# Residues of the weights on VectorE instead of GpSimd while the scans run

## The chip, the cores and the metric

The kernel runs on one core of one Trainium2 chip. The metric is the device time of one execution in microseconds; three runs of the kernel before gave a median of 2983.45 us (2982.43 to 2989.89). Engines are named as in the profile: PE is TensorE's matmuls, PEld its weight loads, DVE is VectorE, ACT is ScalarE, POOL is GpSimd, SP is SyncE, which here only issues DMAs.

## The reference, cut to what matters

One layer of a bidirectional backbone is computed for 1024 latent tokens and 128 context tokens, all in float32, with D_MODEL = 1024:

```
h = rmsnorm(x) * (1 + sc1) + sh1
z = h @ w_in                                  # r, k, v, low-rank inputs, conv inputs, gates
o_a = rwkv_mixer(r, k, v, ...)                # 16 heads x 64, one scan forward, one backward
o_b = cb * seq_conv(cc * cx)                  # gated short convolution
merged = g_a * (o_a @ w_pa) + g_b * (o_b @ w_pb)
x = x + gt1 * (merged @ w_o)
h2 = rmsnorm(x) * (1 + sc2) + sh2
u = seq_conv(h2 @ w_up);  x = x + gt2 * ((silu(u_act) * u_lin) @ w_down)
```

The outputs are the normalised tokens and the final states of the context scans. The scan's step is s = s * w + (s a) b + v k, y = s r, for every head and direction.

## The kernel before, in words

All 1152 tokens are worked on together, in three column tiles of 384. Every large product is a "dense job": one tile of 128 output channels, weights of 8 x 128x128 in two halves of 128x512. TensorE multiplies operands of type `fp32r`, and the kernel keeps float32's precision by splitting each operand in a high part and a residue: `hi` is a copy of the weights to that format (ScalarE, `whi<-wraw`), `lo` is `wraw - hi` (`wlo<-wraw,whi`, the subject of this document), and a product is three matmuls, `hi*hi + hi*lo + lo*hi`. A half's way is: DMA from HBM to `wraw` (issued on GpSimd's queue, two buffers), `whi` on ScalarE, `wlo` (three buffers each), then matmuls. `split_w` records copy and residue, one half at the end of a job's first column tile and one within its last, for the job that comes next.

The jobs stand in one list. First come the products with w_in (`psd<-h` in the profile), 67 tiles and a product with the low-rank gate; then those with w_pb (`psd<-x`), for which the convolution branch is read back and split. A second list has w_pa (`psd<-x` too), after which come w_o (`psd<-mg`), w_up (`psd<-g`) and w_down (`psd<-a`).

Between the matmuls of the first list the scans are woven in. They are cut in 36 items (four pairs of head pairs, nine pieces of 128 tokens). An item's work is a set of streams: `prep` (decays and scaled keys: tiles `thw`, `ak`, `fa`, `bt`, `krk`), `prep2` (Gram matrices `gpb` and `gpk` on TensorE, masked by VectorE into `G`, `E` and `O`), `chain` (a triangular inverse: 31 steps of two VectorE operations, `Xt<-X,Dm` and `X<-X,Xt`, on blocks that a DMA brings as `Dm`), `merge` (`mps`, `RSt`), `scan` (matmuls `px` and `py`, state `Wt`) and `finish` (norm of the head's output, `fps`, `fb`, `fv`, `fg`, `y`). What these need and give goes through HBM by DMAs on SP's queue.

What sets the order is a planner in the program itself. `Clock` has a time `now`, which each matmul moves on by a cost, and one time for each of VectorE ("V"), ScalarE ("A") and GpSimd ("G"). Every recorded instruction adds its cost to its engine's time; a stream goes on when the clock has reached the end of its last piece, and `prep` and `finish` only if the backlog of VectorE and ScalarE is under 1500 or 1000 ns. So a cost that is charged to another engine moves what comes after it on all of them. A scheduler then keeps the order by priorities. The costs of the operation in question, from `tt`, and the place where the engine of the residue is chosen, from `split_w`, `split_eng` and `dense`:

```
s.use(eng, 127 + 1.05 * fsize(out) if eng == "V" else 204 + 2.3 * fsize(out))
...
self.tt(s, lo[:, :nk, :], raw[:, :nk, :], hi[:, :nk, :].bitcast(F32), ALU.subtract, eng=self.split_eng())
...
return self.split
...
self.split = self.split_next          # in dense(), after the first job's two halves
```

The first job's halves go to `split`, the others of that list to `split_next`. After the first list the program sets both to "V" (`K.split = K.split_next = "V"`).

Of the kernel before, what the change touches and what calls it, by code (L numbers as in the profile page):

```python
# [46 lines left out]
class Clock:  # L47


    def __init__(self):  # L50
        self.now = 0.0
        self.e = {"V": 0.0, "A": 0.0, "G": 0.0}
# [24 lines left out]
class Kern:  # L77
    def __init__(self, tc, ins, outs):
        self.tc, self.nc = tc, tc.nc
        self.ins, self.outs = ins, outs  # L80
        self.clk = Clock()
        self.streams = []
        self.events = set()
        self.split, self.split_next = "V", "G"


    def mm(self, out, lhsT, rhs, start, stop, cost):
# [1445 lines left out]
```

## Time and profile before

| | |
|---|---|
| median of three runs | 2983.45 us |
| profiled execution, its own time | 2987.0 us |
| its span in the profile | 2985.1 us |
| mean granted TensorE clock | 0.975 |
| busy: TensorE / weight loads | 2769.4 us (93%) / 2514.1 us (84%) |
| busy: VectorE, ScalarE, GpSimd | 2012.6 us (67%), 1267.4 us (42%), 494.4 us (17%) |
| residues of weights on VectorE / GpSimd | 186 / 148 |
| first and last residue on GpSimd | 13.6 us, 1906.0 us |
| last matmul with w_in | 1805.7 us |

Matmuls are pipelined and their ends are modelled, so a busy TensorE is not one at its peak. A row of groups shows the line, engine, operation, the tiles written and read, partitions x elements, the count, the busy time, the mean of one in ns, and the idle time of the engine ahead of it with what ended it. L110 is the helper `tt`, L105 `act`, L122 `stt`, L89 `mm`, L128 `dma`: most operations have a helper's line, so they are told apart by tiles. A wait is put down to what came last by the profile.

### The profile page before, as it was taken

To read this page: it belongs to the slowest core of one execution; us is meant where nothing else is said; L and a number is where in the kernel's file an instruction comes from. 1 tells how busy PE (TensorE), PEld (TensorE's weight loads), DVE (VectorE), ACT (ScalarE), POOL (GpSimd) and SP (SyncE) were. 2 spreads that over 40 slices of the span, in tenths; PEclk is the share of its full clock that TensorE was granted. 3 is DMA by queue.
4 is the path that set the end of the run, shared out by engine and by line. 5 is a ranking of instruction groups with operands and counts; after the bars stand their busy time and mean duration, and the time that the engine had idled before them with its cause. 6 is when DMAs were issued, how large, how long until landed. Compare 5 with 4: busy or idle time off the path is not lost. (4 is left out here: it accounts for less than half of the span.)

```text
span 2985.1 us, 63295 instructions
## 1 busy us (share of the span) xinstructions
PE 2769.4 (93%) x24762; PEld 2514.1 (84%) x24762; DVE 2012.6 (67%) x5039; ACT 1267.4 (42%) x2544; POOL 494.4 (17%) x678
## 2 busy tenths in 40 slices
PE   7896998999989999889999998999999999999997
PEld 3884887878778777777777788899999999999996
DVE  7457785687667689888887857955555454555556
ACT  4474645555454634334543454123443241424243
POOL 3211121121221111111111112200001101010101
PEclk9997999999999999999999999999999999999998
DMA  4577646466565645545554538843211111111112
GB/s 195 163 238 224 199 148 194 154 175 183 156 185 145 216 109 126 131 109 134 140 139 108 136 115 311 264 141 98 65 43 36 50 40 46 41 41 43 40 44 80
DMA packets 402641, 388.49 MB, mean 130 GB/s; under 512 B 189478, under 2 KB 354214, under 8 KB 402342
## 3 DMA queue, kind: packets, MB, share of 16 engines
q1 hardware_dynamic: 331174, 280.08, 31.1%
q0 software_dynamic: 32000, 99.65, 11.0%
q10 hardware_dynamic: 39168, 4.73, 1.1%
q8 instruction: 195, 3.19, 0.5%
q14 instruction: 104, 0.84, 0.1%
HBM read 268.17 MB, written 116.13 MB: 129 GB/s over the span
## 5 line engine op out<-in xcount | busy, mean ns | idle before, releaser
L89 PE MATMUL psd<-h,whi 128*128 128x384 f32 x3216 | 907.7, 353 | 17.2 <-ACT h L105 9.3
L89 PEld LDWEIGHTS psd<-h,whi 128*128 128x128 f32 x3216 | 591.8, 192 | 52.6 <-issue 12.6
L89 PE MATMUL psd<-h,wlo 128*128 128x384 f32 x1608 | 564.9, 351 | 1.3 <-POOL wlo L110 1.3
L89 PE MATMUL psd<-g,whi 128*128 128x384 f32 (+1 forms) x2112 | 543.2, 338 | 0.0
L105 ACT ACTIVATE whi<-wraw 128x512 fp32r<-128x512 f32 (+2 forms) x334 | 198.3, 594 | 494.3 <-PE psd L89 431.4
L89 PEld LDWEIGHTS psd<-g,whi 128*128 128x128 f32 x2112 | 383.5, 188 | 0.3
L110 POOL TENSOR_TENSOR wlo<-wraw,whi 128x512 fp32r<-128x512 f32 x148 | 199.7, 1350 | 1098.6 <-ACT whi L105 950.9
L89 PE MATMUL psd<-g,wlo 128*128 128x384 f32 (+1 forms) x1056 | 355.9, 337 | 0.0
L89 PEld LDWEIGHTS psd<-h,wlo 128*128 128x128 f32 x1608 | 309.0, 192 | 14.5 <-issue 5.3
L110 DVE TENSOR_TENSOR Xt<-X,Dm 128x60 f32<-128x60 f32 (+24 forms) x1116 | 258.8, 234 | 28.7 <-DMA Dm<-Dd 1.1
L110 DVE TENSOR_TENSOR X<-X,Xt 128x60 f32<-128x60 f32 (+24 forms) x1116 | 253.0, 229 | 27.4 <-DMA O<-fa 0.3
L89 PE MATMUL psd<-a,whi 128*128 128x384 f32 x864 | 218.9, 334 | 0.0
L89 PE MATMUL psd<-x,whi 128*128 128x384 f32 x768 | 200.2, 341 | 10.4 <-ACT x L105 6.7
L89 PEld LDWEIGHTS psd<-g,wlo 128*128 128x128 f32 x1056 | 199.3, 189 | 0.0
L110 DVE TENSOR_TENSOR wlo<-wraw,whi 128x512 fp32r<-128x512 f32 (+2 forms) x186 | 113.7, 611 | 110.6 <-ACT whi L105 110.6
L89 PEld LDWEIGHTS psd<-a,whi 128*128 128x128 f32 x864 | 156.0, 188 | 0.0
L110 DVE TENSOR_TENSOR fu<-psd,rs 128x384 f32<-128x384 f32 x132 | 73.4, 556 | 117.6 <-PE psd L89 105.1
L89 PEld LDWEIGHTS psd<-x,whi 128*128 128x128 f32 x768 | 140.9, 191 | 13.1 <-ACT x L105 7.0
L89 PE MATMUL psd<-a,wlo 128*128 128x384 f32 x432 | 144.0, 334 | 0.0
L122 DVE SCALAR_TENSOR_TENSOR x<-psd,mod,x 128x384 f32<-128x384 f32 (+3 forms) x160 | 79.1, 514 | 94.0 <-PE psd L89 93.9
L105 ACT ACTIVATE BK<-BK,PC 128x128 f32<-128x128 f32 x288 | 94.4, 391 | 108.1 <-PE gpk L89 86.2
L89 PE MATMUL psd<-x,wlo 128*128 128x384 f32 x384 | 130.4, 340 | 4.4 <-DVE wlo L110 4.4
(213 smaller groups left out, 5111.6 us busy)
## 6 DMA issues: line engine op xcount, KB each, us to landing
wraw<-in_w_in POOLq DMA_DIRECT2D x134, 256.0 KB, 3.5
wraw<-in_w_up POOLq DMA_DIRECT2D x88, 256.0 KB, 2.9
llo<-lo SPq DMA_DIRECT2D x98, 192.0 KB, 3.0
BK<-fb SPq DMA_DIRECT2D x36, 512.0 KB, 5.0
Dm<-Dd POOLq DMA_DIRECT2D x144, 128.0 KB, 3.6
wx<-in_wmb SPq DMA_DIRECT2D x32, 512.0 KB, 5.3
fa<-fa SPq DMA_DIRECT2D x40, 384.0 KB, 2.7
fb<-ak SPq DMA_DIRECT2D x40, 384.0 KB, 3.2
```

The lines of the kernel that those rows point to most:

```text
L89: return self.nc.tensor.matmul(out, lhsT=lhsT, rhs=rhs, start=start, stop=stop)
L105: self.nc.scalar.activation(out, in_, func, bias=bias, scale=scale)
L110: e.tensor_tensor(out, a, b, op)
L122: self.nc.vector.scalar_tensor_tensor(out, a, sc, b, op0, op1)
```

## The change

One value is changed: the engine of the residues after the first job of the first list.

```diff
@@ -81,7 +81,7 @@
         self.clk = Clock()
         self.streams = []
         self.events = set()
-        self.split, self.split_next = "V", "G"
+        self.split, self.split_next = "V", "V"
```

All 334 residues are VectorE's then. The planner charges each of the moved ones to VectorE's clock, with VectorE's cost, and so the order of all engines changes from early in the first list on. The number of instructions on the other engines stays, apart from how rows fall together.

On VectorE's queue, in the middle of the scans, the chain of the fifth item (tiles `X` and `Xt`; `cot` is the convolution branch). Before, and with the change:

```order
L110 TENSOR_TENSOR X<-X,Xt 128x28
L110 TENSOR_TENSOR Xt<-X,Dm 128x2x27
L110 TENSOR_TENSOR X<-X,Xt 128x2x27
L110 TENSOR_TENSOR Xt<-X,Dm 128x2x26
L110 TENSOR_TENSOR X<-X,Xt 128x2x26
L110 TENSOR_TENSOR Xt<-X,Dm 128x2x25
```

```order
L110 TENSOR_TENSOR X<-X,Xt 128x28
L110 TENSOR_TENSOR Xt<-X,Dm 128x2x27
L110 TENSOR_TENSOR X<-X,Xt 128x2x27
L110 TENSOR_TENSOR wlo<-wraw,whi 128x512
L110 TENSOR_TENSOR Xt<-X,Dm 128x2x26
L110 TENSOR_TENSOR X<-X,Xt 128x2x26
L110 TENSOR_TENSOR Xt<-X,Dm 128x2x25
```

A residue now stands between two steps of the chain, and what is behind it waits for its `whi`.

On VectorE's queue, at the end of the scans, where the work of `finish` for the last item meets the residues of the activations for w_pb and w_pa (tiles `x`; 17497 and 16655 are of the convolution branch for w_pb, 23256 to 23268 of the scans' output for w_pa) and the modulation's dot products (`wx`). Before, and with the change:

```order
L122 SCALAR_TENSOR_TENSOR fb<-fps,fb 128x128
L122 SCALAR_TENSOR_TENSOR y<-y,par,fb 128x128
L122 SCALAR_TENSOR_TENSOR y<-y,par,fv 128x128
L110 TENSOR_TENSOR fg<-y,fg 128x128
L396 SCALAR_TENSOR_TENSOR wx,mod<-wx 128x1024 x4
L110 TENSOR_TENSOR x_23256<-x_23256,x_23255 128x384 x3
L110 TENSOR_TENSOR x_23259<-x_23259,x_23258 128x384 x3
L110 TENSOR_TENSOR x_23262<-x_23262,x_23261 128x384 x3
L110 TENSOR_TENSOR x_23265<-x_23265,x_23264 128x384 x3
L110 TENSOR_TENSOR x_23268<-x_23268,x_23267 128x384 x3
L110 TENSOR_TENSOR x_17497<-x_17497,x_17496 128x384 x3
```

```order
L122 SCALAR_TENSOR_TENSOR fps<-fps,fb 128x128
L110 TENSOR_TENSOR wlo<-wraw,whi 128x512
L122 SCALAR_TENSOR_TENSOR fb<-fps,fb 128x128
L122 SCALAR_TENSOR_TENSOR y<-y,par,fb 128x128
L110 TENSOR_TENSOR wlo<-wraw,whi 128x512
L110 TENSOR_TENSOR x_16655<-x_16655,x_16654 128x384 x3
L122 SCALAR_TENSOR_TENSOR y<-y,par,fv 128x128
```

The scans end later against the dense jobs: `wx` and the w_pa residues no longer stand ahead of the w_pb residues, but two weight residues do. On TensorE's queue 121 matmuls with w_in stood behind the last matmul of `finish`, and 19 stand there now.

## The prediction

> **What bounds the kernel now.** I read the time by stretches first. The columns are busy time and count of TensorE (PE), its weight loads (PEld), VectorE (DVE), ScalarE (ACT) and GpSimd (POOL), then the granted clock:
>
> ```profile
> core 0: us, PE busy (x) PEld busy (x) DVE busy (x) ACT busy (x) POOL busy (x), PEclk, DMA share, GB/s
> 0.00:200.00 200.00, 165.72 (x712) 127.42 (x713) 120.06 (x194) 105.56 (x191) 56.72 (x66) 0.93 0.56 192
> 200.00:1000.00 800.00, 716.93 (x6716) 627.68 (x6714) 561.78 (x1453) 421.38 (x907) 154.70 (x188) 0.96 0.60 180
> 1000.00:1600.00 600.00, 544.94 (x8401) 454.08 (x8401) 508.01 (x1787) 244.00 (x573) 103.68 (x152) 0.98 0.51 133
> 1600.00:1910.00 310.00, 288.32 (x2960) 260.26 (x2961) 239.64 (x633) 123.46 (x245) 68.98 (x80) 0.97 0.61 190
> 1910.00:2985.00 1075.00, 1053.50 (x5980) 1044.64 (x5978) 583.12 (x977) 372.99 (x628) 110.35 (x192) 0.99 0.20 63
> ```
>
> TensorE is the bound everywhere. From 1910 us on nothing changes: its residues are VectorE's already, and it is 98% full. The change acts ahead of that. In 200 to 1910 us TensorE is idle for 83.1 + 55.1 + 21.7 = 159.9 us; a gain can come from there alone. VectorE is busy for 1309.4 of these 1710 us, idle for 401; it is fullest at 1000 to 1600 us, with 92 us idle in 600. Next, who waits for whom there (total, times, longest); the first rows of TensorE's, then VectorE's and GpSimd's last ones:
>
> ```profile
> PE gpk L89 <- DVE G L110: 16.5, 11, 4.1
> PE px L89 <- DVE Wt L1387: 14.8, 30, 2.3
> PE gpb L89 <- DMA BK<-fb: 14.3, 4, 7.8
> PE gpb L89 <- DMA E<-fa: 13.2, 11, 3.4
> PE lps L89 <- ACT ak L105: 6.8, 3, 3.6
> ...
> PE psd L89 <- POOL wlo L110: 1.3, 1, 1.3
> ...
> PE fps L89 <- DVE y L110: 0.3, 1, 0.3
> ```
>
> All of the view's rows for this stretch add up to 51.8 us for VectorE (20 rows, the first and the last of them above), 50.8 for ScalarE, 44.3 for DMAs, and 1.3 for a GpSimd residue. So the slow residues on GpSimd cost no wait worth naming: what the change can win is not there. It can only make VectorE earlier or later for TensorE.
>
> **The change, part by part.** *Added.* VectorE takes 148 subtractions of 128x512. What one costs there, and what it costs GpSimd, from the groups of the whole run; below them the same tile by stretch (TensorE's use, its loads, VectorE, GpSimd):
>
> ```profile
> L110 DVE TENSOR_TENSOR wlo<-wraw,whi 128x512 fp32r<-128x512 f32 x122 | 84.7, 694 | 80.3 <-ACT whi L105 80.3
> L110 POOL TENSOR_TENSOR wlo<-wraw,whi 128x512 fp32r<-128x512 f32 x148 | 199.7, 1350 | 1098.6 <-ACT whi L105 950.9 <-PE px L89 50.1 <-ACT BK L105 23.2
> 200.00:1000.00 800.00, 282.99 (x813) 155.85 (x812) 0.00 (x0) 91.83 (x68) 0.96 0.60 180
> 1000.00:1600.00 600.00, 147.87 (x411) 78.47 (x411) 0.00 (x0) 44.20 (x34) 0.98 0.51 133
> 1600.00:1910.00 310.00, 127.95 (x374) 70.95 (x374) 0.00 (x0) 43.28 (x31) 0.97 0.61 190
> ```
>
> 148 x 0.694 = 102.7 us more work on VectorE; 133 of the 148 lie in 200 to 1910 us.
>
> *Removed.* GpSimd's 199.7 us, and with them what they do to VectorE. One place in order of time (start, duration), GpSimd's row and then VectorE's:
>
> ```profile
> 702.78 1.29 POOL L110 TENSOR_TENSOR wlo<-wraw,whi 128x512 fp32r<-128x512 f32 x1
> 702.36 0.55 DVE L122 SCALAR_TENSOR_TENSOR kr<-ksq,kr 128x384 f32<-128x384 f32 x1
> 702.83 1.31 DVE L110 TENSOR_TENSOR Xt<-X,Dm 128x52 f32<-128x52 f32 x1
> 704.60 0.20 DVE L110 TENSOR_TENSOR X<-X,Xt 128x52 f32<-128x52 f32 x1
> ```
>
> The step Xt, which starts 0.05 us after the residue, takes 1.31 us and ends 0.07 us after it; its neighbour of the same size takes 0.20. Two operands in SBUF were held up until GpSimd was done. How much that is in all has bounds: nothing, and the 199.7 us for which GpSimd works on residues. Between them, the two operations of the chain (minimum, median and maximum, then the group's mean), and an operation of 128x1024 first beside GpSimd's residues (1830 to 1906 us), then after the last of them (1912 to 1985 us):
>
> ```profile
> L110 DVE TENSOR_TENSOR Xt<-X,Dm x1116: 146/214/1358, 263.8 to 1737.2; 128x60 f32<-128x60 f32 x18, 128x28 f32<-128x28 f32 x14, 128x48 f32<-128x48 f32 x12, 128x54 f32<-128x54 f32 x12
> L110 DVE TENSOR_TENSOR X<-X,Xt x1116: 160/211/1431, 264.0 to 1737.9; 128x60 f32<-128x60 f32 x18, 128x28 f32<-128x28 f32 x14, 128x48 f32<-128x48 f32 x12, 128x54 f32<-128x54 f32 x12
> L110 DVE TENSOR_TENSOR Xt<-X,Dm 128x60 f32<-128x60 f32 (+24 forms) x1116 | 258.8, 234 | 28.7 <-DMA Dm<-Dd 1.1
> L110 DVE TENSOR_TENSOR X<-X,Xt 128x60 f32<-128x60 f32 (+24 forms) x1116 | 253.0, 229 | 27.4 <-DMA O<-fa 0.3
> L396 DVE SCALAR_TENSOR_TENSOR wx<-wx 128x1024 f32<-128x1024 f32 x39 | 54.6, 1399 | 3.0 <-DMA wx<-in_wmb 2.2
> L396 DVE SCALAR_TENSOR_TENSOR wx<-wx 128x1024 f32<-128x1024 f32 x18 | 22.0, 1221 | 0.3
> L110 DVE TENSOR_TENSOR G<-gpb,mask 128x512 f32<-128x512 f32 x72 | 49.1, 682 | 24.5 <-PE gpk L89 16.4 <-PE gpb L89 5.0 <-DMA G<-Xd 2.9
> ```
>
> Mean less median, times the count: 1116 x (20 + 18) ns = 42 us in 511.8 us of chain. Spread over VectorE's 1309.4 us of that stretch it would be 108 us; but G, which reads one operand from PSUM, is as fast there as an undisturbed subtraction of 512, so I take 95 us, an estimate. Net, VectorE gets 102.7 - 95 = 8 us more (bounds: 97 less, 103 more). Nearly each us given to it is one that it lost already, and mostly at the same places.
>
> The Trainium skill says so in two pages. "SBUF — State Buffer", section "Who interferes with whom", has a VectorE instruction with two SBUF inputs and a GpSimd instruction that reads SBUF lock each other out for the whole instruction; the place above agrees. "Perfetto Trace Analysis", section "Optimizing Scalar/DVE Operations", draws from the shared port that moving work between those two "might not help"; by it the time would not change, as I forecast below.
>
> *What of it reaches the end.* VectorE's waits in 200 to 1910 us come to 330.7 us, over 43 rows whose costliest are
>
> ```profile
> DVE Wt L1387 <- ACT Wt L105: 40.8, 34, 3.3
> DVE ak L110 <- ACT ak L105: 24.9, 16, 4.1
> DVE ksq L116 <- PE kps L89: 24.4, 6, 6.2
> DVE thw L1145 <- ACT thw L105: 22.7, 20, 2.2
> DVE y L122 <- PE fps L89: 19.1, 10, 8.7
> ```
>
> With the 95 us, 426 us make VectorE late, and TensorE waits 51.8 us for it: a share of 0.12. All later terms go by it. The 8 us give +1 us (bounds -12 and +12).
>
> *New waits.* A residue on VectorE stands in its queue behind ScalarE's `whi` copy, and what is behind it (the chain, the state's copies `Wt`, the masks G, E, O, for all of which TensorE waits) stands with it. On GpSimd that wait, 950.9 us of the row above, held up weight loads and `Dm` alone. The trace has no such wait in the scans; its nearest rows are the residues after the scans and the one small residue of the same form in them (200 to 1910 us):
>
> ```profile
> L110 DVE TENSOR_TENSOR wlo<-wraw,whi 128x512 fp32r<-128x512 f32 (+2 forms) x186 | 113.7, 611 | 110.6 <-ACT whi L105 110.6
> L110 DVE TENSOR_TENSOR lwlo<-lwraw,lwhi 64x512 fp32r<-64x512 f32 x6 | 4.1, 682 | 10.2 <-ACT lwhi L105 10.2
> ```
>
> 110.6 / 186 = 0.59 us and 10.2 / 6 = 1.7 us for each; below them, nothing, where the copy is always done. 133 residues wait 78 or 226 us; times 0.12, +9.5 or +27 us. I take the first: it is the very operation, 186 times, while `lwlo` is the first work of a new step and its copy comes right ahead of it.
>
> *The order.* The planner put instructions by its own clock, and that changes with the change. Before, it charged VectorE nothing for a residue, though one cost it 95 / 148 = 0.64 us; now it charges 127 + 1.05 x 512 = 665 ns of 694. For a chain operation of 60 elements it charges 190 ns, and undisturbed medians are 214 and 211: 50 us too little over 2 x 1116. So VectorE ran 95 + 50 = 145 us behind the plan, and will run 50 + 4 = 54 us behind it: 63% of the lag goes. If TensorE's 51.8 us of waits went with it, that is -33 us; if a new order brings new waits for the DMAs and ScalarE, nothing. I take a third, -11 us, since the plan starts afresh at each wait and the other engines' lag stays. The later place of the scans costs nothing: the last of their matmuls now has 19 dense ones behind it ahead of the w_pb products, before 121, and what it feeds is needed only after those products. The w_pb stage has VectorE full, with 7 us of TensorE idle:
>
> ```profile
> 1850.00:1930.00 80.00, 72.99 (x410) 71.27 (x409) 77.89 (x122) 7.59 (x12) 20.17 (x20) 0.99 0.87 289
> ```
>
> There 16 residues add 11 us, and the `wx` rows alone lose 39 x 0.178 = 7 us; with the `wx` work now spread further back, I put it at 0 (plus or minus 4).
>
> *DMA queues.* The loads of `wraw` and `Dm` stay on GpSimd's queue and now wait for VectorE to free a buffer; after 1910 us they do so already, at no idle of TensorE that the table shows. 0.
>
> Sum: +1 + 9.5 - 11 + 0 + 0 = -0.5 us, on the profiled execution's 2987.0 us (span 2985.1). That execution is 3.5 us above the median shown, 2983.45; on the median's scale I forecast **2983 us**, no change. About 0.3%, 9 us, is what a measurement of this kernel can tell from none.
>
> **Rivals.** *The queue stands (slower).* Residues wait 1.7 us as `lwlo` does, and the new order brings no relief: +1 + 27 = +28, **3011 us**. For it: at 1000 to 1600 us VectorE has 92 us idle, and 34 x (0.69 + 1.7) = 81 us less what it loses no longer would fill most of that. Against: `thw`, `ak` and `Wt`, which wait for ScalarE too, lose about 1 us a wait and not each time. It is slower by over 9 us from a mean wait of 1.25 us on (133 x 1.25 x 0.12 = 20, less the 11).
>
> *The plan fits better (faster).* All of the -33 us, and waits of 0.2 us (+3): +1 + 3 - 33 = -29, **2954 us**. For it: the largest wait, G, is of a VectorE operation behind the chain, where the blocked operations sit. Against: 95 of TensorE's 147 us of named waits are for ScalarE and DMAs, and a better VectorE doesn't touch them.
>
> *The lock is worth all it can be (faster).* Every residue blocks VectorE for its whole 1.35 us: 97 us less on VectorE, -12 us beside the forecast's terms, **2971 us**. That is the first page's rule taken to its end. Against: G's 682 ns and the chain's medians.
>
> That the change does nothing of what it says is out: the built program has no residue left on GpSimd.
>
> **How the numbers follow.** No change 0.37, the queue 0.32, the better plan 0.25, the full lock 0.06. The forecast's own range is 2973 to 2993 (bounds of the 8 us and of the w_pb stage, and a new order's luck). The range for 8 in 10 reaches to both sides' rivals: 2953 to 3012. Same: three quarters of the first case and a little of each neighbour, 0.33; slower: the queue less a tenth, and an eighth of the first case, 0.33; faster: the other two and the last eighth, 0.34.
>
> **What would show it.** VectorE's busy time within 15 us of 2012.6; the maximum of Xt and X in the scans down from 1.36 and 1.43 us to about 0.3, and medians as now; the residues' wait for `whi` in 200 to 1910 us at 0.59 us each, against 1.25 and more for the queue; TensorE's waits for VectorE near 50 us, against some 20 for the better plan. I am wrong in the mechanism if VectorE's chain operations stay stretched without GpSimd's residues, or if TensorE comes to wait for `wlo` itself in the scans.

## The result, and the profile after

The changed kernel takes 2936.64 us, the median of five runs (2931.55 to 2942.27), against 2983.45 for the kernel before (2982.29 to 2990.31): a ratio of 0.9826, 95% interval 0.9800 to 0.9851. That is 47 us or 1.7% faster, outside of the predicted range (2953 to 3012). The profiled execution took 2936.6 us, its span 2934.9 us, at a mean granted clock of 0.978 (0.975 before).

Where the time went, by stretches of the changed kernel, in the columns of the prediction's table:

```profile
0.00:200.00 200.00, 170.28 (x758) 130.21 (x758) 124.92 (x212) 109.73 (x201) 36.68 (x52) 0.96 0.57 195
200.00:1000.00 800.00, 724.28 (x6761) 634.14 (x6763) 569.74 (x1539) 435.83 (x937) 62.73 (x121) 0.95 0.62 186
1000.00:1600.00 600.00, 558.20 (x8737) 469.12 (x8733) 504.25 (x1870) 239.81 (x561) 62.51 (x124) 0.98 0.51 130
1600.00:1860.00 260.00, 246.68 (x2500) 220.26 (x2500) 191.39 (x559) 113.91 (x220) 20.60 (x40) 0.99 0.61 191
1860.00:2935.00 1075.00, 1056.23 (x6017) 1047.93 (x6015) 601.37 (x1012) 373.86 (x630) 110.94 (x193) 0.99 0.21 68
```

From 1860 us on the table reads as before from 1910 us on, within 3 us of TensorE's busy time. So the gain lies ahead of that, and nearly all of it in the scans: in the first 200 us TensorE is idle for 29.7 us instead of 34.3. From 200 us to that point it is idle for 75.7 + 41.8 + 13.3 = 130.8 us, before 159.9, and busy for 1529.2 us, before 1550.2. The last matmul with w_in begins at 1762.5 us instead of 1805.9.

What TensorE waits for in 200 to 1860 us (total, times, longest), the first rows, and those on the weights' two parts:

```profile
PE gpb L89 <- DMA E<-fa: 16.0, 13, 2.4
PE gpk L89 <- DVE G L110: 12.8, 12, 3.5
PE gpb L89 <- issue: 11.5, 3, 5.5
PE px L89 <- DVE Wt L1387: 11.3, 28, 1.4
...
PE psd L89 <- DVE wlo L110: 4.9, 2, 4.7
...
PE psd L89 <- ACT whi L105: 1.1, 1, 1.1
```

All rows of that view: 43.7 us for VectorE (51.8 before), 27.8 for ScalarE (50.8), 41.0 for DMAs (44.3), 12.4 for nothing that the profile names (4.6). So the waits put down to ScalarE fell most, though no work of ScalarE was touched; VectorE's fell by 8 us. Next the groups on VectorE, with mean ns and the idle time ahead of them, and the two operations of the chain (minimum, median, maximum):

```profile
L110 DVE TENSOR_TENSOR wlo<-wraw,whi 128x512 fp32r<-128x512 f32 (+2 forms) x334 | 215.1, 644 | 145.9 <-ACT whi L105 143.6 <-PE px L89 0.9 <-ACT x L105 0.8
L110 DVE TENSOR_TENSOR Xt<-X,Dm 128x60 f32<-128x60 f32 (+24 forms) x1116 | 229.6, 209 | 25.5
L110 DVE TENSOR_TENSOR X<-X,Xt 128x60 f32<-128x60 f32 (+24 forms) x1116 | 228.6, 208 | 25.4 <-DVE X L110 0.2
L396 DVE SCALAR_TENSOR_TENSOR wx<-wx 128x1024 f32<-128x1024 f32 x64 | 78.2, 1221 | 4.5 <-DMA wx<-in_wmb 3.7
L110 DVE TENSOR_TENSOR G<-gpb,mask 128x512 f32<-128x512 f32 x72 | 49.1, 682 | 34.2 <-PE gpk L89 28.7 <-PE gpb L89 3.5 <-DMA G<-Xd 1.8
L110 DVE TENSOR_TENSOR Xt<-X,Dm x1116: 132/213/241, 269.4 to 1712.8; 128x60 f32<-128x60 f32 x18, 128x28 f32<-128x28 f32 x14, 128x54 f32<-128x54 f32 x13, 128x48 f32<-128x48 f32 x12
L110 DVE TENSOR_TENSOR X<-X,Xt x1116: 145/210/240, 269.6 to 1713.0; 128x60 f32<-128x60 f32 x18, 128x28 f32<-128x28 f32 x14, 128x54 f32<-128x54 f32 x13, 128x48 f32<-128x48 f32 x12
```

The chain's maxima are 0.24 us instead of 1.36 and 1.43, its two groups take 458 us instead of 512, and every `wx` takes 1221 ns. G, with one operand in PSUM, is 682 ns as it was. In 200 to 1860 us alone the residues read

```profile
L110 DVE TENSOR_TENSOR wlo<-wraw,whi 128x512 fp32r<-128x512 f32 x131 | 89.7, 685 | 27.4 <-ACT whi L105 25.0 <-PE px L89 0.9 <-ACT x L105 0.8
```

so the new wait for `whi` is 25.0 / 131 = 0.19 us each. I also added up, over every VectorE instruction that overlaps an arithmetic operation of GpSimd, its duration less the median of its like (same line, tiles and shape): 105.3 us before, and 8.6 after, at the start and the end of the program. GpSimd's residues blocked VectorE for some 97 us.

### The profile page after: what moved, and what is told of

It is laid out like the page before. It is cut to its first block, busy times and chain, and to the rows that moved or that the text cites. A ratio compares the mean times of both kernels' runs of the same rounds, so it can differ in the third digit from the quotient of the medians.

```text
span 2934.9 us, 63331 instructions
## 1 busy us (share of the span) xinstructions
PE 2755.7 (94%) x24762; PEld 2501.7 (85%) x24762; DVE 1991.7 (68%) x5187; ACT 1273.1 (43%) x2548; POOL 293.5 (10%) x530
## 4 chain that ended last, share of the span: by engine, by line
PE 66%; DVE 13%; DMA 12%; ACT 4%; issue 3%; SPq 2%; ACTq 0%; POOL 0%; DVEq 0%; POOLq 0%
PE psd L89 53%; PE px L89 3%; SPq L128 2%; DMA E<-fa 2%; DVE X L110 2%; DVE Xt L110 2%; PE mps L89 2%; PE fps L89 1%; PE gpb L89 1%; PE py L89 1%; PE gpk L89 1%; PE lps L89 1%; DMA BK<-fb 1%; PE bps L89 1%; DVE ak L110 1%
## 5 line engine op out<-in xcount | busy, mean ns | idle before, releaser
L110 DVE TENSOR_TENSOR wlo<-wraw,whi 128x512 fp32r<-128x512 f32 (+2 forms) x334 | 215.1, 644 | 145.9 <-ACT whi L105 143.6
L110 DVE TENSOR_TENSOR Xt<-X,Dm 128x60 f32<-128x60 f32 (+24 forms) x1116 | 229.6, 209 | 25.5
L110 DVE TENSOR_TENSOR X<-X,Xt 128x60 f32<-128x60 f32 (+24 forms) x1116 | 228.6, 208 | 25.4 <-DVE X L110 0.2
L128 POOL DMA_DIRECT2D wraw<-in_w_in x134 | 73.7, 550 | 1165.2 <-DVE wlo L110 562.3
L122 DVE SCALAR_TENSOR_TENSOR x<-psd,mod,x 128x384 f32<-128x384 f32 (+3 forms) x160 | 78.9, 514 | 92.9 <-PE psd L89 92.8
```

Source lines behind the costliest of these rows:

```text
L110: e.tensor_tensor(out, a, b, op)
L122: self.nc.vector.scalar_tensor_tensor(out, a, sc, b, op0, op1)
L128: q.dma_start(out=out, in_=in_)
```

## The experiments

All 18 are compared with the kernel before on the same chip, so a ratio may be set beside any other; within a set the microseconds may be too (the first four rows, the next four, the four of `fix`, the four of `ord`, the last two). Spans and clocks are of one execution each.

| run | what it is | median, us | ratio to before (95%) | span, us / clock |
|---|---|---|---|---|
| e1_planV_runG | planner charges VectorE, GpSimd runs it | 3016.97 | 1.0104 [1.0071, 1.0137] | 3008.6 / 0.969 |
| e2_planG_runV | planner charges GpSimd, VectorE runs it | 2928.00 | 0.9802 [0.9768, 0.9837] | 2918.1 / 0.983 |
| e3_also_pool_reads | after, GpSimd subtracts too | 3011.59 | 1.0078 [1.0049, 1.0107] | 3003.3 / 0.972 |
| e4_also_pool_memset | after, GpSimd as long, only writing | 2947.95 | 0.9865 [0.9835, 0.9895] | 2943.5 / 0.976 |
| e5_also_dve | after, each residue twice on VectorE | 2930.94 | 0.9789 [0.9751, 0.9827] | 2915.5 / 0.982 |
| e7_no_residue | the moved residues left out | 2930.12 | 0.9784 [0.9757, 0.9811] | 2919.9 / 0.982 |
| p1_before | before, another gate for `prep` | 2998.10 | 1.0019 [0.9999, 1.0038] | 2995.7 / 0.975 |
| p2_before | before, other latencies in the planner | 3002.01 | 1.0029 [1.0007, 1.0051] | 3009.2 / 0.971 |
| fix_none | e7 with its order frozen | 2926.46 | 0.9791 [0.9768, 0.9813] | 2921.1 / 0.982 |
| fix_V | that order, residues on VectorE | 2963.69 | 0.9906 [0.9877, 0.9936] | 2960.9 / 0.977 |
| fix_VV | that order, twice on VectorE | 3014.02 | 1.0077 [1.0062, 1.0093] | 3010.5 / 0.969 |
| fix_G | that order, residues on GpSimd | 2993.53 | 1.0004 [0.9991, 1.0017] | 2995.1 / 0.969 |
| ordV_runV | order laid for VectorE, run there | 2931.59 | 0.9800 [0.9771, 0.9830] | 2929.9 / 0.979 |
| ordV_runG | order laid for VectorE, run on GpSimd | 2978.44 | 0.9972 [0.9952, 0.9992] | 2976.4 / 0.973 |
| ordG_runV | order laid for GpSimd, run on VectorE | 2965.91 | 0.9916 [0.9891, 0.9941] | 2964.6 / 0.977 |
| ordG_runG | order laid for GpSimd, run there | 2985.63 | 0.9997 [0.9980, 1.0014] | 2982.7 / 0.974 |
| v_all | e2 and GpSimd's other reads on VectorE | 2908.32 | 0.9734 [0.9711, 0.9756] | 2901.0 / 0.985 |
| e2_again | e2 once more, beside v_all | 2935.81 | 0.9823 [0.9799, 0.9847] | 2927.8 / 0.982 |

### Is it the planner, or where the work runs?

Two kernels separate the planner's charge from the engine. In the first the planner charges VectorE as after and GpSimd runs the residues; the second is the other way round (`on_next` is "G" or "V", `split_next` the other).

```diff
-        self.split, self.split_next = "V", "V"
+        self.split, self.split_next = "V", "V"; self.on, self.on_next = None, "G"
...
-        e = self.nc.vector if eng == "V" else self.nc.gpsimd
+        e = self.nc.vector if (on or eng) == "V" else self.nc.gpsimd
```

> The planner charges the residues to VectorE as in the changed kernel, but they run on GpSimd as before. Lock theory (GpSimd's residues stop VectorE's two-operand instructions, and TensorE and ScalarE feel it): about 2980 us, between 2970 and 2995, since the residues are where they were. Plan theory (what helped is that the planner's clock now knows of the residue): about 2940 us. Both by half: about 2960.

> The planner charges the residues to GpSimd as before, but they run on VectorE. Lock theory: about 2940 us, since nothing holds VectorE up any more. Plan theory: about 2980 us, VectorE gets 103 us of work that the plan knows nothing of. Both by half: about 2960.

With GpSimd the charge to VectorE cost 31 us (3016.97 against 2986.08 for before on that chip); with VectorE it costs 0.03% to 0.24%, 1 to 7 us, which the intervals don't tell from nothing (0.9826 after, 0.9802 and 0.9823 without it). The longest step `Xt` of the chain takes 1.43 us in the first kernel and 0.24 in the second. Both theories missed the first (2970 to 2995 and 2940 us were expected), and why the charge costs 31 us there was not settled. But where the residues run decides, and a planner that charges VectorE rightly gains nothing. The order isn't held here: the scheduler laid it anew for each kernel.

### Does GpSimd's reading do it, or its being busy?

Both kernels are the changed one with something for GpSimd to do on the weight buffer after its last use: the same subtraction once more (it reads two operands), or three memsets.

```diff
+        if self.also:
+            self.nc.gpsimd.tensor_tensor(raw[:, :nk, :], raw[:, :nk, :], hi[:, :nk, :].bitcast(F32), ALU.subtract)
```

```diff
+        if self.also:
+            for _ in range(3):
+                self.nc.gpsimd.memset(raw[:, :nk, :], 0.0)
```

> The changed kernel, and behind each moved residue GpSimd does the subtraction once more, into the weights' own buffer, which nothing reads after that. VectorE keeps its 103 us and GpSimd's reads of SBUF are back. Lock theory: the chain's longest operations are at 1.3 us again, VectorE's busy time rises by about 95 us, and the time to 2980 us or more. Plan theory: about 2940 us. Queue theory (a GpSimd that is busy issues the loads of weights late): as the next kernel.

> The same with three memsets of that buffer on GpSimd, which keep it busy as long (about 1.3 to 1.6 us) but read nothing. Lock theory: the chain's operations stay under 0.3 us, and about 2940 us. Queue theory: 2965 us or more. Plan theory: about 2940 us.

GpSimd's own group and the chain in the first, the reading one:

```profile
L227 POOL TENSOR_TENSOR wraw<-wraw,whi 128x512 f32<-128x512 f32 x148 | 215.2, 1454 | 1134.5 <-DVE wlo L110 1016.3 <-issue 54.6 <-ACT e L105 24.9
L110 DVE TENSOR_TENSOR Xt<-X,Dm x1116: 145/212/1720, 274.1 to 1780.9; 128x60 f32<-128x60 f32 x17, 128x28 f32<-128x28 f32 x13, 128x48 f32<-128x48 f32 x13, 128x66 f32<-128x66 f32 x13
```

And in the second, the writing one:

```profile
L228 POOL MEMSET wraw<- 128x512 f32 x444 | 232.2, 528 | 1049.9 <-DVE wlo L110 962.5 <-issue 53.4 <-ACT Wt L105 16.5
L110 DVE TENSOR_TENSOR Xt<-X,Dm x1116: 144/212/418, 272.9 to 1731.8; 128x60 f32<-128x60 f32 x17, 128x28 f32<-128x28 f32 x14, 128x48 f32<-128x48 f32 x13, 128x66 f32<-128x66 f32 x13
```

GpSimd is as busy in both (215 and 232 us) and holds the weight buffer as long. Beside the reads `Xt` is stretched to 1.72 us, and the kernel is 75 us slower than the changed one; beside the memsets it stays at 0.42 us, and the kernel is 11 us slower, an interval that overlaps with the changed kernel's. By the sum over medians as above, less the 8.6 us that the changed kernel has too, the reads block VectorE for 104 us and the memsets for nothing. So the late weight loads, which both have, are worth some 11 us, and the reading 64 us. In these 64 us there is a difference of order, for the scheduler laid the two kernels differently; two experiments below say how much an order can be worth. The Trainium skill, page "SBUF — State Buffer", section "Who interferes with whom", says that a VectorE instruction with two SBUF inputs contends with a GpSimd instruction that reads SBUF, not with one that only writes it; both halves agree here.

### What does the work itself cost on VectorE?

The moved residues were left out (the third matmul of a tile then takes the high part of the weights, so the result is another), or made twice (the second into the weight buffer after its last use).

```diff
-            self.tt(s, lo[:, :nk, :], raw[:, :nk, :], hi[:, :nk, :].bitcast(F32), ALU.subtract, eng=self.split_eng())
+            lo = hi
```

```diff
+        if self.also:
+            self.nc.vector.tensor_tensor(raw[:, :nk, :], raw[:, :nk, :], hi[:, :nk, :].bitcast(F32), ALU.subtract)
```

> The changed kernel without the moved residues: the high part stands in for the residue, so the third matmul of each product multiplies by it; matmuls, loads and copies are as many. The planner charges nothing for them. No blocking and no work on VectorE. Share theory: 103 us less than the changed kernel's work at the price of the blocking, so some 65 us below it, about 2870 us. Placement theory: 2915 to 2935 us, as the kernel that runs them on VectorE without the planner's charge.

> The changed kernel, with each moved residue computed a second time on VectorE, into the weights' own buffer, which nothing reads after that: 103 us more work on VectorE, of which the planner is told nothing, while the instructions stand in the queue as the scheduler puts them. If an us of VectorE is an us of VectorE, however it is lost (share theory), this costs what the GpSimd copies cost: their 95 to 110 us of blocking gave +65 to +75 us, so about 3000 us. If work that stands in the queue fits in gaps and blocking doesn't (placement theory), 2940 to 2960 us.

Busy times of the two, without residues and with twice as many:

```profile
PE 2737.6 (94%) x24762; PEld 2496.1 (85%) x24762; DVE 1915.5 (66%) x5039; ACT 1267.8 (43%) x2544; POOL 294.2 (10%) x530
```

```profile
PE 2747.8 (94%) x24762; PEld 2499.2 (86%) x24762; DVE 2066.5 (71%) x5335; ACT 1262.1 (43%) x2539; POOL 294.1 (10%) x530
```

VectorE is busy for 151 us more in the second, and the times are 2930.12 and 2930.94 us. That is against the theory of one share for all lateness (about 2870 and 3000 us). Queued work on VectorE cost nothing; some 97 us of blocking had cost about 50. Two reasons were open. The scheduler may lay the other engines' order around work that it knows of, and can't for blocking (theory K below); or blocking is dear by itself (theory C).

### Is it luck of the order?

Two kernels are the one before with a small change in the planner (the gate of `prep` at 1200 instead of 1500 ns; a stream's latencies 20 ns longer), for other orders without any other cause.

```diff
-        K.spawn(prep_all, 3, gate=1500, ahead=1000)
+        K.spawn(prep_all, 3, gate=1200, ahead=1000)
```

```diff
-        self.t = max(self.t, start + cost + (260 if eng == "A" else 120))
+        self.t = max(self.t, start + cost + (280 if eng == "A" else 140))
```

> The kernel before with one planner constant changed (the backlog from which the prep stream holds back, 1500 to 1200): the order shifts a little, by 11 dense matmuls in the mean. It measures what a new order by itself is worth. If the gain of the change is luck of the order: several tens of us either way. Lock theory: 2975 to 2995 us.

> The kernel before with the planner's latencies raised by 20 ns (120 to 140 and 260 to 280): the order shifts by 46 dense matmuls in the mean, nearer to the changed kernel's (29 from it) than to its own, and the scans end about as late as there; the residues stay on GpSimd. Order theory (the later place of the scans is what helped): about 2940 us. Lock theory: 2975 to 3015 us.

They are 0.2% and 0.3% slower than the kernel before, the first 3 us over what I had allowed: two other orders don't bring what the change brought. It is not luck of the kind that they sample.

### One frozen order, residues on either engine

Here the program is laid out twice. The first pass gives the order of every engine's instructions as the scheduler chose it without residues; the second writes that order into the program as fixed and puts the residues in, the only instructions that may float.

```diff
+    nc, seen = made("none")
...
+                    for p, q in zip(idx, idx[1:]):
+                        tc.add_manual_dep(seen[e][q], seen[e][p].name, mybir.DependencyInfo(
+                            mybir.DependencyClass.NoSync, mybir.DependencyReason.DATA), reason="order")
...
+    nc, _ = made(MODE, {e: v for e, v in order.items() if e in FIXED})
```

The order of TensorE, ScalarE and SyncE is the same in all four, and so is VectorE's and GpSimd's but for the residues. (Rows of small matmuls that run side by side, and of DMA issues on ScalarE, change places in the traces by a few tenths of a us.)

> The base of a set with one frozen order. The moved residues are left out (the third matmul of each tile takes the high part of the weights, so the result is another), as in the kernel without the residues, and the order of the instructions of every engine, as the scheduler chose it for that kernel, is then written into the program as fixed. Both theories expect the time of that kernel, 2930 us, within 6 us, since the orders are the same row by row; another time would say that fixing the order costs something by itself, and the other three of the set would be read against it.

> The frozen order of the kernel without residues, and the 148 residues put back on VectorE, where the order of TensorE, ScalarE, SyncE and the rest of VectorE does not make room for them. Theory K (an amount of work on VectorE costs nothing only because the scheduler knows of it and lays the other engines' work around it; work or blocking that it does not know of costs 0.6 of itself): 103 us on VectorE unknown to the order cost 60 us, 2990 us. Theory C (what makes the blocking dear is that it strikes the short instructions of the scan chain in the middle of their work, and queued work of 0.65 us a piece is absorbed whether it is known or not): 2930 to 2945 us.

> As the last, with each of the 148 residues made twice in a row on VectorE: 206 us of VectorE work that the frozen order does not know of. Theory K: 2930 + 0.6 x 206 = 3050 us. Theory C: 2930 to 2960 us, since pieces of 1.3 us begin to reach the 1.4 us of the blocked instructions.

> As the frozen order with the residues on VectorE, the same order row by row on TensorE, ScalarE and SyncE, but the 148 residues on GpSimd. Both theories expect some 60 us over the kernel without residues, 2990 to 3000 us; what is told apart is its distance to the frozen order with the residues on VectorE: Theory K none (within 10 us), Theory C 50 us or more. A GpSimd time of 2930 to 2945 us here would let both fall and put the price on the order that the scheduler makes for GpSimd.

Freezing costs nothing (0.9791, and 0.9784 for the same kernel unfrozen). What the residues take on VectorE, once and twice:

```profile
L228 DVE TENSOR_TENSOR wlo<-wraw,whi 128x512 fp32r<-128x512 f32 x148 | 101.3, 686 | 47.3 <-ACT whi L105 46.5
L229 DVE TENSOR_TENSOR wlo<-wraw,whi 128x512 fp32r<-128x512 f32 x296 | 201.6, 686 | 47.4 <-ACT whi L105 45.6
```

In an order that has no room for them, the 148 residues take 101.3 us on VectorE and cost 37.2 us (a share of 0.37); twice as many take 201.6 us and cost 87.6 (0.43). Both times lie between what the two theories expected. So one part of the explanation holds: work is free on VectorE where the order was laid with it, and not where it wasn't. On GpSimd the residues cost 67.1 us. The busy times of the pair, first on VectorE:

```profile
PE 2753.5 (93%) x24762; PEld 2508.2 (85%) x24762; DVE 1999.9 (68%) x5187; ACT 1266.2 (43%) x2544; POOL 293.4 (10%) x530
```

and on GpSimd, in the same order:

```profile
PE 2772.7 (93%) x24762; PEld 2523.1 (84%) x24762; DVE 2013.6 (67%) x5039; ACT 1266.5 (42%) x2544; POOL 497.0 (17%) x678
```

VectorE is busy for 2000 and 2014 us: the blocking takes nearly as much of its time as the work. Yet GpSimd costs 30 us more than VectorE at one order. Neither theory had that: K expected no more than 10, C 50 and more.

### Order and engine crossed

The same construction, with the order laid for residues on VectorE or for residues on GpSimd (the planner charges them to no engine), and each order run both ways. On VectorE's, GpSimd's and SyncE's queues the first order is that of e2_planG_runV instruction by instruction, and the second that of the kernel before.

```diff
-    nc, seen = made("none")
+    nc, seen = made("V")
```

> The order of all engines as the scheduler lays it with the 148 residues on VectorE (the planner charges them to no engine), frozen, and the residues on VectorE. Both theories: as the changed kernel, 2925 to 2940 us. The base of the crossed set.

> The same order as the last row by row on TensorE, ScalarE and SyncE, laid for 103 us of residues on VectorE, but the residues run on GpSimd. If blocking is dear only because no order is laid for it (theory K): the room for 103 us on VectorE takes the 100 us of blocking up, 2940 to 2955 us. If it is dear by itself (theory C): 2990 to 3000 us, as the order without residues gave.

> The order as laid for the residues on GpSimd, frozen, and the residues on VectorE, where the order leaves no room for them. Both theories: some 37 us over the order laid for VectorE, 2960 to 2975 us, as the order without residues gave; 2930 to 2940 us would say that an order for VectorE's residues is worth nothing, and that the 37 us belonged to that one order.

> The order as laid for the residues on GpSimd, frozen, and the residues on GpSimd: the kernel before but for the planner's charge. Both theories: 2985 to 3000 us, as the kernel before. Its distance to the run with the same order and the residues on VectorE is the price of GpSimd at one order: theory K at most 10 us (blocking and work cost alike where the order knows neither), theory C 25 us or more.

| | run on VectorE | run on GpSimd | price of GpSimd |
|---|---|---|---|
| order laid for VectorE | 2931.6 | 2978.4 | 46.9 |
| order laid for GpSimd | 2965.9 | 2985.6 | 19.7 |
| order laid without residues | 2963.7 | 2993.5 | 29.8 |

The whole change is 54 us here (2985.6 to 2931.6), and both parts are needed. At the old order the engine is worth 20 us and the new order then 34; the other way round the new order is worth 7, which the intervals don't tell from nothing, and the engine 47. An order laid for 103 us of VectorE work doesn't take up the blocking: that run came out 23 us over what theory K allowed, and 12 under theory C's. Both fall as they stood. At every order GpSimd is dearer than the same work on VectorE, so part of the price is in running there; and a fitting order takes most of the rest off, but only where the work runs as laid.

Where the price of GpSimd is at one order can be read from two sums: TensorE's waits by the profile (all rows of that view, whole run), and what half clock took from TensorE, (1 - clock) x span. The second is an estimate: half-clock time in which TensorE idles is in it too.

| from, to | span, us | TensorE's waits, us | of them for ScalarE / VectorE / DMAs | lost to the clock, us |
|---|---|---|---|---|
| ordV_runV, ordV_runG | +46.5 | 162.4, 184.9 | 42.6, 57.8 / 48.0, 55.3 / 62.2, 61.4 | 61.5, 80.4 |
| ordG_runV, ordG_runG | +18.1 | 182.3, 193.9 | 55.7, 72.8 / 61.6, 66.0 / 53.3, 45.3 | 68.2, 77.6 |
| fix_V, fix_G | +34.2 | 189.8, 205.2 | 61.1, 68.5 / 62.7, 70.6 / 55.2, 49.6 | 68.1, 92.8 |
| after, before | +50.2 | 160.4, 196.9 | 49.9, 76.1 / 46.6, 57.9 / 47.9, 53.2 | 64.6, 74.6 |

Waits and clock together give 41, 21, 40 and 47 us of 47, 18, 34 and 50. TensorE's busy time says the same without the clock: it grows by 23, 7 and 19 us in the three pairs of one order. So about half of the price at one order is a slower TensorE. These are single executions, and the clock differs among them: e2_planG_runV and ordV_runV have one order, but 101 and 125 us at half clock. Before has 27 stretches at a granted clock of 0.5, 151 us in all, each of 3.4 us or a multiple of it but the last; the run without residues has 18, 108 us in all. The Trainium skill, "TensorE: Matmul & The Clock Gate", Part 1, has TensorE fall to half clock after an idle window of about 3.4 us. The lengths agree. But of the 3.4 us just ahead of a stretch TensorE is idle, before, for only 2.2 us in the median (0.5 to 3.4), so a window needn't be wholly idle here; which wait starts which stretch was not settled. Most of the waits that GpSimd adds are put down to ScalarE in the crossed pairs, not to VectorE. One row of ScalarE's own waits up to 1910 us looks as if it said why. In the order laid for VectorE, with the residues on GpSimd:

```profile
ACT whi L105 <- PE psd L89: 121.1, 43, 10.4
ACT whi L105 <- issue: 30.2, 26, 3.1
```

and with them on VectorE:

```profile
ACT whi L105 <- PE psd L89: 161.4, 78, 13.5
ACT whi L105 <- issue: 1.3, 1, 1.3
```

With GpSimd the `whi` copies wait 30.2 us for something that the profile doesn't name. But the wait for TensorE's products is 40 us shorter there, and all rows of `whi` come to 180.4 and 178.1 us (198.1 before, 194.0 after): the wait has changed its name and not its length. So the row shows no delay of ScalarE, and why TensorE waits more for ScalarE stays open.

### GpSimd's other reads

At the start and the end of the program GpSimd still has arithmetic: 12 of 24 products of `xT`, 8 of 24 low parts of `h`, 4 residues of the last down projection, 6 products of the last norm. All of it goes to VectorE, on top of the second kernel above (the 6 products in one instruction with their scaling, which ScalarE did).

```diff
-                    K.tt(S0, xT[m][:, sl], xT[m][:, sl], rstd[:, sl], ALU.mult, eng="VVG"[t] if t != 1 else "GV"[m % 2])
+                    K.tt(S0, xT[m][:, sl], xT[m][:, sl], rstd[:, sl], ALU.mult, eng="V")
...
-                         eng="GV"[m % 2] if t else "V")
+                         eng="V")
...
-                    if m in (1, 4):
+                    if m in ():
...
-                    K.tt(s, lo[:, :nk], raw[m][:, :nk], hi[:, :nk].bitcast(F32), ALU.subtract, eng="VG"[m % 2])
+                    K.tt(s, lo[:, :nk], raw[m][:, :nk], hi[:, :nk].bitcast(F32), ALU.subtract, eng="V")
```

> The kernel that plans the residues for GpSimd and runs them on VectorE, and the last subtractions and products on GpSimd moved to VectorE as well: 12 of the 24 products of xT, 8 of the 24 low parts of h, 4 residues of the last down projection, 6 products of the last norm. If GpSimd's reads block VectorE there as in the scans, two engines gain nothing over one: the 24 products of xT took 15 us, 12 on each engine at 1.2 us each, and take 24 x 0.47 = 11.3 us on VectorE alone; in all 3 to 8 us faster than its base. If the two engines work side by side, VectorE gets 30 more operations of 0.5 us in stages with nothing beside them: 5 to 10 us slower than its base.

> The base of the run before, once more: 2925 to 2932 us, as it was.

The 24 products on two engines (minimum, median, maximum in ns, first and last start):

```profile
L110 POOL TENSOR_TENSOR xT<-xT,rstd x12: 989/1302/1310, 41.0 to 54.6; 128x384 f32<-128x384 f32 x12
L110 DVE TENSOR_TENSOR xT<-xT,rstd x12: 882/1344/1347, 41.3 to 55.0; 128x384 f32<-128x384 f32 x12
```

and on VectorE alone:

```profile
L110 DVE TENSOR_TENSOR xT<-xT,rstd x24: 556/564/568, 41.1 to 52.3; 128x384 f32<-128x384 f32 x24
```

From the first start to the last, two engines took 14 us where one takes 11: they do not run side by side, each VectorE product lasts as long as GpSimd's beside it. The base came out at 2935.8 us, above the 2932 that I allowed, at a ratio within the interval of its first run. The kernel is 27 us faster than its base on the same chip, 2908.3 us, and the fastest of all: 0.9734 [0.9711, 0.9756] of the kernel before. I had expected 3 to 8 us. The low parts of `h` begin their last one at 76.2 us instead of 82.2, which is 6 us; the last matmul with w_in begins at 1724.6 instead of 1747.9, so some 17 us more are won from there to the end of the scans, in which no instruction changed its engine and the order was laid anew. TensorE's waits are 147.2 us instead of 165.3 and the clock 0.985 instead of 0.982 (43.5 and 52.7 us lost). Why the scans gain is not settled.

## Why the prediction was wrong, point by point

- *The bound and the place* were right in the main. TensorE bounds, and of 50 us all but some 5 came from 200 us to the end of the scans: 29 from TensorE's idle time, the rest from its busy time. Those 5 lie in the first 200 us, which the prediction had left out.
- *The work added*, 102.7 us on VectorE, was right (685 to 694 ns each).
- *The blocking removed*, 95 us between bounds of 0 and 199.7, was right: some 97 by the traces, though 95 was a choice between 42 and 108. The chain's maxima went to 0.24 us as written, and the operations of 128x1024 to 1221 ns. Undisturbed medians were the right base for it.
- *VectorE's net time* went down by 20.9 us (2012.6 to 1991.7), not up by 8, 6 us outside of the 15 that I allowed. The sum of all durations did go up, by 3 us (2180.2 to 2182.8), as the two terms above have it. But rows that follow each other overlap by some 0.08 us in the profile, and busy time counts that once: 191 us of overlap after, 168 before. So 23 of the 29 us between are a matter of counting.
- ***What of it reaches the end* is the step that failed**: the share of 0.12, and that one share served for everything. It was TensorE's waits for VectorE over VectorE's own lateness. The runs have three prices in its place: 0 for work on VectorE that the order was laid with (none, once and twice the residues: 2930, 2928 to 2937, 2931 us), 0.37 to 0.43 for work that the order has no room for, and 0.6 to 0.7 for blocking, with all that goes with it on GpSimd (67 us for 100 us of it at the order without residues; 64 us for 104 us between added reads and memsets, at two orders). Taking work and blocking off against each other to "8 us net", at one price, hid a change of some 50 us. The waits of before could not give these prices. Their 0.12 is a mean over lateness that the order was laid with: in the frozen order 101 us more work raised TensorE's waits for VectorE by 25 us (37.3 to 62.7) and the time by 37. And where the residues leave GpSimd, most of the fall stands under another name: 23 of the 28 us by which the waits fell in the scans stood under ScalarE, for which no run shows the reason, and at one order a slower TensorE adds about as much again as the waits. My test "waits for VectorE near 50 us" came near (43.7) and said nothing.
- *New waits* were over-sized: 0.19 us each instead of 0.59; by the share of 0.12, +3 us instead of +9.5. The queue rival, which needed 1.25 us, falls; its price was far off in any case. TensorE waited for `wlo` itself 4.9 us, twice. I had named that as a sign of a wrong mechanism; at this size it decides nothing.
- *The order* had the wrong cause. I gave -11 us to the planner's clock; charging VectorE cost 31 us with GpSimd and 1 to 7 us with VectorE. (The term had a slip, too: it set the charge of a step of 60 elements against medians over all sizes. Step by step the 2232 charges fall 70 us short and not 50, which makes it -9.) But the order that the scheduler lays with the residues on VectorE is worth 34 us when they run there, and 7 when they don't. The term was too small, for a reason that I hadn't considered.
- *DMA queues* at 0: no run tests the term by itself; the run with memsets puts late loads at some 11 us. *The w_pb stage*: it is as long as it was, as forecast (214.7 and 214.9 us from its first matmul to the last with w_pa).
- *The rivals.* "The plan fits better", 2954 us, was nearest in time and had the wrong mechanism; had the time come out there, it would have been luck. "The full lock" had the right one, but took it to the end in the blocked time (which the forecast had right) instead of in its price.
- The sentence of the Trainium skill, "Perfetto Trace Analysis", "Optimizing Scalar/DVE Operations", that moving work between these two engines "might not help" does not describe this case: the move gave 1.7%, and moving the rest another 0.9%. The Trainium skill's page "SBUF — State Buffer", named in the same paragraph of the prediction, is the one that the runs bear out.

With the measured prices the sum is -20 for the engine at the old order, -34 for the order laid with the work, and +1 to +7 for the planner's charge: -47 to -53 us, measured -47. That is a division of what was measured, not a forecast that was tested on another kernel.

## What to carry to other kernels

A unit of time on an engine has no single price: here, work that the order was laid with cost nothing and blocking more than half of itself, so they must not be netted against each other. Where VectorE shows short two-operand instructions that end with a GpSimd instruction, first take the GpSimd reads away; on this kernel that is worth more than the 100 us of VectorE time that it costs. And TensorE's waits for one engine needn't show what that engine's lateness costs, here 8 us less under VectorE's name of 47 us gained: add up the waits under all names, for a name can change while the sum stays, and look at the granted clock too.

## What the runs showed of the hardware that I had not expected

- What half clock takes is no small part of this kernel: (1 - clock) x span is 43.5 us in the fastest version and 93 us in the slowest of the frozen orders. It moves with the waits: at one order 12 to 23 us more of waits came with 9 to 25 us more lost to the clock.
- GpSimd memsets of 232 us in all left VectorE's chain at a maximum of 0.42 us, while reads of 215 us stretched it to 1.72.
- Two engines on 24 products of two SBUF operands took longer (14 us from the first start to the last) than VectorE alone (11 us).
- 148 x 0.69 us more work in the queue of an engine that is 66% busy, and as much again, did not change the time by more than the runs differ among themselves, where the order was laid with that work.
